# One dense transformer block on one core: where the gate-and-up stage makes its operand sums, and what is prepared before each stage begins

## The chip, the cores and the metric

The kernel runs on one core of a Trainium2 chip. The metric is the device time of one execution in microseconds (us); the times of the kernel before are from three runs. The engines are TensorE (PE: matmul, with its weight load PEld), VectorE (DVE), ScalarE (ACT), GpSimd (POOL) and SyncE (SP), which here issues nearly all DMAs.

## The reference

One layer over 2048 latent tokens of width 1024, with 256 context tokens in front: a modulated norm, one input projection shared by gated linear attention and differential attention, an output projection, and a gated feed-forward part of hidden width 2816. All of it is float32. The change touches what stands behind the attention:

```python
def swiglu(h, w_in, w_out):
    gate, up = jnp.split(h @ w_in, 2, axis=-1)
    return (jax.nn.silu(gate) * up) @ w_out
...
x = x + gt1 * (mixed @ w_out)
x = x + gt2 * swiglu(modulate(x, norm2_g, sh2, sc2), w_ffn_in, w_ffn_out)
```

(The last two lines are a short form.)

## The kernel before, in words

Every float32 operand is split in two: `split` lets ScalarE copy the value in reduced precision (`hi`, line 87) and VectorE subtract that from it (`lo`, line 84). A product is then three matmuls (`mm3`, lines 91 to 93: hi·hi, hi·lo, lo·hi), mostly 128x128 stationary by 512 moving columns. The helper `mul` is line 78, `add` line 81, `sub` line 84, whichever engine runs them. On TensorE instructions stand in the order of the code (`manual_schedule`); on the other engines a scheduler orders them, and each engine works through its list in order. Tiles come from pools with a fixed number of buffers, so a load or a split waits until the earlier user of its buffer is done.

Stages 1 to 3 (projections, linear attention, differential attention; to about 1519 us) are not edited.

*Output projection* (lines 897 to 1066). The eight 128x1024 chunks of `w_out` are loaded, multiplied by the gate `gt1` on GpSimd and split. `main(lt)` computes one token tile, from lt = 15 down to 0: two halves of 512 columns, each 8 chunks of `mm3`, taken in the order 4, 5, 6, 7, 0, 1, 2, 3. Between its chunks `prep` makes the next tile's operand (norms, transposes) and `mod2(g)` the normalised, transposed input `h2` of the feed-forward part for two token tiles. Groups 4 to 7 stay on chip in the blocks `hb`, groups 0 to 3 are stored. `mod2(0)`, the last, runs behind the last `main`. `early_ops` makes slot 0 and two sums.

*Gate and up* (lines 1068 to 1153). Tokens in two halves of 1024; for each half 22 blocks of 128 hidden columns. A block is a two-by-two product (gate and up by two token groups of 512; two halves of the inner dimension of 1024) done with seven products instead of eight. The moving operands are slots `o0` to `o6`, 128x2048 each, hi and lo: four pieces of `hb` and three sums, made by `rest_ops` before the half's first block. The stationary operands are seven 128x512 pieces `wh`, `wl`: three pieces of the weight tile `wi` and four sums of them (`s2`, `s3`, `a21`), which GpSimd makes. A product is 4 x `mm3` = 12 matmuls into a PSUM bank `p`; VectorE and ScalarE combine the banks to gate and up in tiles `e`, `g` and store the result to `act`. A block is 84 matmuls, the stage 44 x 84 = 3696.

*Down stage* (lines 1155 to 1192). For each half of the 1024 output columns (`dd`) the 22 weight chunks `wo` are loaded, multiplied by the gate `gt2` (GpSimd and VectorE in turn) and split into `wot`; for each of 16 token tiles `ar` (128x2816) is loaded from `act`, split into `ah`, `al`, and 22 x `mm3` = 66 matmuls with 512 columns make one result, to which `x1t` is added (2 x 16 x 66 = 2112 matmuls). The pool of `wot` has 22 + 6 buffers, that of `wo` 4.

Of the kernel before, what the change touches and what calls it, by code (L numbers as in the profile page):

```python
# [11 lines left out]
F32 = mybir.dt.float32  # L12
# [21 lines left out]
GA, GB, EQB, DEFER = 2, 5, 2, 4  # L34
PREP, MOD = (0, 7, 13), (1, 8, 10, 12, 14)
# [14 lines left out]
def dit_block(ctx: ExitStack, tc: tile.TileContext, x, c, cx, c_ctx, w_mod, b_mod, norm1_g, w_in, gate_up,  # L50
# [839 lines left out]
    with ExitStack() as st:  # L890
# [25 lines left out]
        wo = [tuple(wp.tile([P, D], F32R, name=f"wo{u}_{k}") for u in "hl") for k in range(KT)]  # L916
        for k in range(KT):
            w = xp.tile([P, D], F32, name="xt", tag="xt")
            load(w, w_out[0, k * P:(k + 1) * P, :])
            mul(w, w, gt1, G)  # L920
            split(wo[k][0], wo[k][1], w)
        def gla_out(lt, mixt):
# [141 lines left out]
        for _ in mod2(0):  # L1064
            pass
# [3 lines left out]
        SEQ_P = ((0, 0, True), (1, 1, True), (0, 2, False), (2, 3, True), (3, 4, True), (2, 5, False), (3, 6, False))  # L1069
# [6 lines left out]
        ep = st6.enter_context(tc.tile_pool(name="s5e", bufs=2, side="right", reuse_waits="tile"))  # L1076
# [155 lines left out]
```

## Time and profile before

| | |
|---|---|
| time, median of three runs | 3206.38 us (3201.48, 3206.38, 3211.32) |
| time of the profiled execution | 3207.87 us |
| its span, first to last instruction | 3206.1 us |
| mean granted TensorE clock | 0.977 of full speed |
| busy share: PE, DVE, ACT, POOL | 96%, 67%, 44%, 25% |

The profile shows one execution. A busy share is a mean over all stages; what an edit in one stage can give is read from that stage's own stretch. Times in the views count from the first instruction of the span. "Released by" names the instruction whose end let another one begin.

### The profile page before, as it was taken

The page shows a single profiled execution, that of the slowest core. Times are in us where ns is not written, and L with a number is a line of the kernel's source. Part 1 is how long each engine was busy: PE and PEld are TensorE (multiplying, and loading weights), DVE is VectorE, ACT ScalarE, POOL GpSimd, SP SyncE. Part 2 cuts the span into 40 slices and gives each one's busy share as a digit, 9 for nine tenths or more (in the row PEclk, how much of TensorE's full clock was granted, in tenths as well). Part 3 has the DMA queues.
Part 4 walks back from the last instruction along what each step waited for, and adds up shares of the span by engine and source line. Part 5 has one row for each costly group of instructions (what it writes and reads, how often), then busy time and mean ns, then how long its engine had stood idle before and what let it go on. Part 6 is the DMA issues. An engine that isn't in the chain of part 4 may idle for free.

```text
span 3206.1 us, 41971 instructions
## 1 busy us (share of the span) xinstructions
PE 3061.8 (96%) x15124; PEld 2497.9 (78%) x15124; DVE 2144.5 (67%) x4608; ACT 1411.2 (44%) x2169; POOL 796.0 (25%) x506
## 2 busy tenths in 40 slices
PE   7999999999989999999699799998999997999999
PEld 4888788888867777777588588887788885887787
DVE  7888668878899999998786744446554445323322
ACT  5333466666567777776333333334233333212211
POOL 2111000000056556654321322222322222100000
PEclk9999999999999999999899899999999998999999
DMA  8965511211332222211556332222222325434331
GB/s 307 302 225 200 165 68 66 93 63 62 95 83 65 63 66 57 57 52 45 176 169 199 110 87 86 79 79 65 74 80 83 87 73 180 153 135 158 125 136 66
DMA packets 316769, 363.46 MB, mean 113 GB/s; under 512 B 25361, under 2 KB 258258, under 8 KB 305810
## 3 DMA queue, kind: packets, MB, share of 16 engines
q1 hardware_dynamic: 313970, 351.35, 34.4%
q0 software_dynamic: 2304, 8.39, 0.8%
q8 instruction: 119, 1.95, 0.2%
q10 hardware_dynamic: 288, 1.05, 0.1%
q14 instruction: 88, 0.72, 0.1%
HBM read 249.96 MB, written 110.76 MB: 113 GB/s over the span
## 4 chain that ended last, share of the span: by engine, by line
PE 64%; DVE 3%; DMA 2%; POOL 1%; issue 1%; ACT 1%; SPq 0%; POOLq 0%; DVEq 0%; ACTq 0%
PE p L93 9%; PE p L92 9%; PE p L91 9%; PE o L92 6%; PE o L93 6%; PE o L91 6%; PE t L818 4%; PE s L773 4%; PE s L774 4%; PE o L841 3%; PE mm L92 2%; PE mm L91 2%; PE mm L93 2%; DMA wo<-in_w_ffn_out 1%; POOL p L81 0%
## 5 line engine op out<-in xcount | busy, mean ns | idle before, releaser
L81 POOL TENSOR_TENSOR p<-p,p 128x1152 f32<-128x1152 f32 x128 | 366.3, 2882 | 289.7 <-DVE p L805 174.7
L775 DVE TENSOR_SCALAR_CACHE_REDUCE p<-s 128x512 f32<-128x512 f32 (+1 forms) x640 | 382.0, 631 | 13.5 <-PE s L774 9.5
L91 PE MATMUL mm<-wh,hh 128*128 128x512 f32 (+2 forms) x976 | 379.0, 388 | 0.0
L93 PE MATMUL mm<-wh,hl 128*128 128x512 f32 (+2 forms) x976 | 355.0, 364 | 0.1
L92 PE MATMUL mm<-wl,hh 128*128 128x512 f32 (+2 forms) x976 | 354.4, 363 | 0.0
L81 DVE TENSOR_TENSOR e<-p,e 128x512 f32<-128x512 f32 x220 | 152.1, 691 | 279.9 <-PE p L93 279.9
L781 ACT ACTIVATE p<-p,nm 128x2304 f32<-128x2304 f32 x128 | 283.8, 2217 | 44.5 <-DVE nm L779 44.5
L91 PE MATMUL o<-wot,ah 128*128 128x512 f32 x704 | 279.6, 397 | 19.7 <-ACT wot L87 19.6
L92 PE MATMUL o<-wot,ah 128*128 128x512 f32 x704 | 280.2, 398 | 8.7 <-DVE wot L84 8.7
L773 PE MATMUL s<-k,qh 128*128 128x512 f32 (+1 forms) x640 | 275.7, 435 | 9.6 <-DVE p L775 8.7
L93 PE MATMUL o<-wot,al 128*128 128x512 f32 x704 | 278.0, 395 | 0.0
L87 ACT ACTIVATE wh<-wi 128x512 fp32r<-128x512 f32 x176 | 111.1, 632 | 326.0 <-PE p L92 247.3
L774 PE MATMUL s<-k,ql 128*128 128x512 f32 (+1 forms) x640 | 234.4, 373 | 1.3 <-DMA ql<-ql 1.3
L87 ACT ACTIVATE ah<-ar 128x2816 fp32r<-128x2816 f32 x32 | 81.9, 2559 | 327.5 <-PE o L92 312.1
L84 POOL TENSOR_TENSOR s<-wi 128x512 f32<-128x512 f32 x88 | 113.7, 1292 | 427.6 <-DVE wl L84 419.4
L93 PEld LDWEIGHTS mm<-wh,hl 128*128 128x128 f32 x976 | 185.1, 190 | 30.2 <-DVE hl L84 0.5
L91 PEld LDWEIGHTS mm<-wh,hh 128*128 128x128 f32 x976 | 186.1, 191 | 23.1 <-issue 0.5
L81 DVE TENSOR_TENSOR x1t<-o,x1t 128x512 f32<-128x512 f32 x32 | 22.1, 691 | 271.3 <-PE o L93 271.3
L92 PEld LDWEIGHTS mm<-wl,hh 128*128 128x128 f32 x976 | 186.1, 191 | 21.4 <-issue 0.5
L87 ACT ACTIVATE wh<-s 128x512 fp32r<-128x512 f32 x132 | 83.4, 632 | 247.1 <-PE p L92 231.0
L84 DVE TENSOR_TENSOR wl<-s,wh 128x512 fp32r<-128x512 f32 x132 | 93.1, 705 | 126.1 <-ACT wh L87 125.9
L91 PEld LDWEIGHTS o<-wot,ah 128*128 128x128 f32 x704 | 134.6, 191 | 52.9 <-ACT wot L87 24.8
(287 smaller groups left out, 7557.9 us busy)
## 6 DMA issues: line engine op xcount, KB each, us to landing
wi<-in_w_ffn_in SPq DMA_DIRECT2D x88, 512.0 KB, 5.4
ar<-act SPq DMA_DIRECT2D x32, 1408.0 KB, 5.8
act<-e SPq DMA_DIRECT2D x88, 256.0 KB, 2.6
wm<-in_w_mod SPq DMA_DIRECT2D x32, 512.0 KB, 5.0
xt<-in_x SPq DMA_DIRECT2D x30, 512.0 KB, 3.9
wr<-in_w_in SPq DMA_DIRECT2D x12, 1024.0 KB, 7.5
wo<-in_w_ffn_out SPq DMA_DIRECT2D x44, 256.0 KB, 3.8
hdh<-hh SPq DMA_DIRECT2D x9, 1024.0 KB, 4.8
```

Of the source, the lines that this page charges most:

```text
L81: (eng or V).tensor_tensor(out=o, in0=a, in1=b, op=ALU.add)
L84: (eng or V).tensor_tensor(out=o, in0=a, in1=b, op=ALU.subtract)
L87: S.activation(hi, src, AF.Copy)
L91: T.matmul(ps, a[0], b[0], start=start, stop=False, **how)
L92: T.matmul(ps, a[0], b[1], start=False, stop=False, **how)
L93: T.matmul(ps, a[1], b[0], start=False, stop=stop, **how)
L773: T.matmul(ps[:, 0:n], qd[0][c_][:, qc], ks_[h, c_][:, o0:o0 + n], start=True, stop=False)
L774: T.matmul(ps[:, 0:n], qd[1][c_][:, qc], ks_[h, c_][:, o0:o0 + n], start=False, stop=True)
L775: V.tensor_scalar(out=pr[c_][:, o0:o0 + n], in0=ps[:, 0:n], scalar1=1.0, scalar2=-3.0e38, op0=ALU.mult, op1=ALU.max, accum_out=mx[:, j:j + 1])
L781: S.activation(pr[c_], pr[c_], AF.Exp, bias=nm, accum_out=l)
L818: T.transpose(pt[:, i, :], as_[bi][i][:, kt * P:(kt + 1) * P], ident)
L841: T.matmul(po[:, 0:nq, :], v[0], at[0], start=kt == 0, stop=kt == NKT - 1)
```

## The change

- *Output projection.* The first half of the columns takes the chunks in the order 4, 5, 6, 7, 0, 1, 2, 3, the second in the order 3, 2, 4, 5, 6, 7, 0, 1, and the loads are issued in the first of these orders. The pool of the split weights moves to the other side of the memory, below the pools of loads and sums. Two pads shift the tiles of this stage.
- *Before gate and up.* `early_ops` makes slots 0 and 1; its two sums go from GpSimd to VectorE. `mod2(0)` is gone from the end of the stage: `last_group` does its work inside the second block of gate and up, from `x1` read back from memory.
- *Gate and up.* All sums, of weights and of token blocks, are on VectorE. The code makes a product's weights three products ahead (`AHEAD`), with 7 instead of 6 pairs of buffers. The slots of the first half are made one by one ahead of their products; those of the second half are rebuilt one by one, slot i right after product i of the first half's last block (n = 21). The second half runs its column blocks in reverse, and its first block uses the weights of the block before again. The pad ahead of the weight pools grows from 24 to 56 floats for each partition. In the built programs the weight tiles `wh`, `wl` began 384 bytes past a multiple of 512 in a partition, and begin 256 past one after; the slots begin 256 past one in both. The tiles `wot`, `ah`, `al` of the down stage before begin 256 past one as well.
- *Down stage.* Two token tiles are worked on together, so that each weight chunk serves 6 matmuls in a row instead of 3; `ar` comes in halves of 11 chunks (128x1408). The gate `gt2` is no longer multiplied into the weights but, on VectorE, into each result. Weights of the second `dd` are made in the pairs 5 and 7.

Of the diff, the core:

```diff
+ORD0, ORD1 = (4, 5, 6, 7, 0, 1, 2, 3), (3, 2, 4, 5, 6, 7, 0, 1)
+PAD4 = 16
+AHEAD = 3
...
-        slots = {0: slot(sl0, 0)}
+        slots = {i: slot(sl0, i) for i in range(2)}
...
+        pad = st1.enter_context(tc.tile_pool(name="s4pad", bufs=1, side="right"))
+        G.memset(pad.tile([P, 56], F32, name="pad"), 0.0)
...
+        pad = st1.enter_context(tc.tile_pool(name="s4pad2", bufs=1, side="right"))
+        G.memset(pad.tile([P, PAD4], F32, name="pad"), 0.0)
         ph = st1.enter_context(tc.tile_pool(name="s4h", bufs=2, side="right", reuse_waits="tile"))
-        wp = st1.enter_context(tc.tile_pool(name="s4w", bufs=1, side="right", reuse_waits="tile"))
+        wp = st1.enter_context(tc.tile_pool(name="s4w", bufs=1, reuse_waits="tile"))
...
-        wo = [tuple(wp.tile([P, D], F32R, name=f"wo{u}_{k}") for u in "hl") for k in range(KT)]
-        for k in range(KT):
+        wo = {k: tuple(wp.tile([P, D], F32R, name=f"wo{u}_{k}") for u in "hl") for k in ORD1}
+        for k in ORD0:
...
-            order = (4, 5, 6, 7, 0, 1, 2, 3)
-            for j in range(2):
+            for j, order in enumerate((ORD0, ORD1)):
...
                 for k in order:
-                    mm3(ps, (mh[:, k, :], ml[:, k, :]), (wo[k][0][:, js], wo[k][1][:, js]), k == 4, k == 3)
-                    if k == 3:
+                    mm3(ps, (mh[:, k, :], ml[:, k, :]), (wo[k][0][:, js], wo[k][1][:, js]), k == order[0], k == order[-1])
+                    if k == order[-1]:
                         add(x1[:, js], ps, xt[:, js])
...
         def early_ops():
-            split(slots[0][0], slots[0][1], hb[0][0])
-            sub(hb[0][1], hb[1][1], hb[0][1], G)
-            add(hb[0][0], hb[0][0], hb[0][1], G)
+            (b11, b12), (b21, b22) = hb
+            split(*slots[0], b11)
+            sub(b12, b22, b12)
+            add(b11, b11, b12)
+            split(*slots[1], b11)
...
-        for _ in mod2(0):
-            pass
...
-        G.memset(pad.tile([P, 24], F32, name="pad"), 0.0)
+        G.memset(pad.tile([P, 56], F32, name="pad"), 0.0)
         rwp = st6.enter_context(tc.tile_pool(name="s5r", bufs=2, side="right", reuse_waits="tile"))
-        opp = st6.enter_context(tc.tile_pool(name="s5w", bufs=6, side="right", reuse_waits="tile"))
+        opp = st6.enter_context(tc.tile_pool(name="s5w", bufs=7, side="right", reuse_waits="tile"))
...
-        def rest_ops(hb, slots, first):
-            (b11, b12), (b21, b22) = hb
-            if not first:
-                slots[0] = slot(sl0, 0)
-                sub(b12, b22, b12, G)
-                split(*slots[0], b11)
+        def rebuild(blocks, i, fresh):
+            (b11, b12), (b21, b22) = blocks
+            if fresh:
+                slots[i] = slot(sl0 if i < 2 else sl1, i)
+            if i == 1 and fresh:
                 add(b11, b11, b12)
-            for i, src in ((1, b11), (2, b21), (3, b12), (4, b12), (5, b21), (6, b22)):
-                if i == 4:
-                    sub(b12, b22, b11, V if first else G)
-                if i == 5:
-                    sub(b21, b21, b11, G)
-                slots[i] = slot(sl1, i)
-                split(*slots[i], src)
...
+            if i == 4:
+                sub(b12, b22, b11)
+            if i == 5:
+                sub(b21, b21, b11)
+            split(*slots[i], (b11, b11, b21, b12, b12, b21, b22)[i])
+
+        def last_group():
+            xt = h2p.tile([P, 2, D], F32, name="lx", tag="hb00")
+            xn = h2p.tile([P, 2, D], F32, name="lxn", tag="hb01")
+            ht = h2p.tile([P, KT, 256], F32, name="lht", tag="hb10")
+            ss = tmp.tile([P, 2], F32, name="lss", tag="lss")
+            for t in range(2):
+                load(xt[:, t, :], x1_d[t])
+            for t in range(2):
+                S.activation(xn[:, t, :], xt[:, t, :], AF.Square, accum_out=ss[:, t:t + 1])
+            rs = rms_rstd(tmp, ss, D, 2, "l")
+            for t in range(2):
+                V.tensor_scalar(out=xn[:, t, :], in0=xt[:, t, :], scalar1=rs[:, t:t + 1], scalar2=None, op0=ALU.mult)
+            yield
...
+                if kp % 2:
...
+        work = [(1, j) for j in range(NH)] + [(0, j) for j in reversed(range(NH))]
+        raws, kept, sums = {}, {}, {}
...
+        def weights(n, i):
+            if n == NH:
+                return
...
+            a11, s2, a12, s3, a21, a22, _ = sums[n]
+            if i == 1:
+                s2 = tmp.tile([P, 4, P], F32, name="s2", tag="s2")
+                s3 = tmp.tile([P, 4, P], F32, name="s3", tag="s3")
+                sub(s3, a11, a21)
+                add(a21, a21, a22)
+                sub(s2, a21, a11)
+                sums[n] = a11, s2, a12, s3, a21, a22, s2
+            if i == 6:
+                sub(s2, a12, s2)
+            kept[n, i] = [opp.tile([P, 4, P], F32R, name=f"w{u}", tag=f"w{u}") for u in "hl"]
+            split(*kept[n, i], sums[n][i])
+
+        banks, e = [None] * 4, {}
...
+            wh_, wl_ = kept[n - 1, i] if n == NH else kept[n, i]
+            for k in range(4):
...
+        flat = [(n, i) for n in range(len(work)) for i in range(7)]
         with tc.manual_schedule(engines=MS):
-            for half in (1, 0):
-                rest_ops(hb, slots, half == 1)
...
-                    sub(s3, a11, a21, G)
-                    add(a21, a21, a22, G)
-                    sub(s2, a21, a11, G)
...
-                            sub(s2, a12, s2, G)
-                            srcs[6] = s2
-                        wh_, wl_ = wsplit(srcs[i])
...
+            fetch(0)
+            fetch(1)
+            for m in range(AHEAD):
+                weights(*flat[m])
+            late = last_group()
+            for m, (n, i) in enumerate(flat):
+                if n == 0 and i < 5:
+                    rebuild(hb, i + 2, True)
+                if m + AHEAD < len(flat):
+                    weights(*flat[m + AHEAD])
+                if n == 1 and i < 6:
+                    next(late, None)
+                if n == 3 and i == 0:
+                    hb0 = h2_blocks()
+                    for k in range(2):
+                        for b in range(2):
+                            load(hb0[k][b], h2_d[k][b])
+                if n == 6 and i == 0:
+                    sub(hb0[0][1], hb0[1][1], hb0[0][1])
+                ps = product(n, i)
+                finish(n, i, ps)
+                if n == NH - 1:
+                    rebuild(hb0, i, True)
+                if i == 6 and n + 2 < len(work) and n + 2 != NH:
+                    fetch(n + 2)
...
+        downs, chunks = {}, {}
...
+        def down_weights(dd, j):
+            w = wrp.tile([P, 512], F32, name="wo", tag="wo")
+            load(w, w_fo[0, j * P:(j + 1) * P, dd * 512:(dd + 1) * 512])
+            wt = wop.tile([P, 2, 512], F32R, name="wot", tag="wot")
+            split(wt[:, 0], wt[:, 1], w)
...
+            load(ar, act_d[lt // 8][lt // 4 % 2][:, lt % 4, c_ * HC:(c_ + 1) * HC])
+            chunks[lt, c_] = [acp.tile([P, HC, P], F32R, name=f"a{u}", tag=f"a{u}") for u in "hl"]
+            split(*chunks[lt, c_], ar)
...
+        pairs = [(dd, lt) for dd in range(2) for lt in (*range(8, 16, 2), *range(0, 8, 2))]
...
-                    n += 1
-                    ar = pool.tile([P, NH, P], F32, name="ar", tag="ar")
-                    load(ar, act_d[lt // 8][lt // 4 % 2][:, lt % 4])
-                    ah, al = [pool.tile([P, NH, P], F32R, name=f"a{u}", tag=f"a{u}") for u in "hl"]
-                    split(ah, al, ar)
...
-                        for j in range(NH):
-                            w = wrp.tile([P, 512], F32, name="wo", tag="wo")
...
-                            mul(w, w, gt2[:, js], G if j % 2 else V)
-                            wt = wop.tile([P, 2, 512], F32R, name="wot", tag="wot")
-                            split(wt[:, 0], wt[:, 1], w)
...
+                ps, x1t = [], []
+                for t in range(2):
...
+                for c_ in range(2):
...
+                    if n == 0:
+                        for j in range(c_ * HC, (c_ + 1) * HC):
+                            down_weights(0, j)
...
+                    nx = (n, 1) if c_ == 0 else (n + 1, 0)
+                    if nx[0] < len(pairs):
+                        for t in range(2):
+                            tokens(pairs[nx[0]][1] + t, nx[1])
+                    for j in range(c_ * HC, (c_ + 1) * HC):
+                        ah, al = zip(*[chunks[lt + t, c_] for t in range(2)])
+                        for t in range(2):
+                            mm3(ps[t], (ah[t][:, j - c_ * HC, :], al[t][:, j - c_ * HC, :]), downs[dd, j], j == 0, j == NH - 1)
+                        if n == 5 and j < 6:
+                            down_weights(1, j)
+                        if n == 7 and j + 6 < NH:
+                            down_weights(1, j + 6)
+                for t in range(2):
+                    o = op_.tile([P, 512], F32, name="ot", tag="ot", bufs=2)
+                    mul(o, ps[t], gt2[:, js])
+                    add(x1t[t], o, x1t[t])
+                    store(out[0, (lt + t) * P:(lt + t + 1) * P, js], x1t[t])
```

Where instructions go, at three places. On SyncE, between attention and output projection (`md`, `mx`, `on` belong to the attention's result; `xt` are load buffers), before:

```order
L960 DMA mx<-md_13_203 128x128
L860 DMA md_0_238<-on 128x128
...
L860 DMA md_3_241<-on 128x128
L960 DMA mx<-md_13_219 128x128
...
L960 DMA mx<-md_13_251 128x128
L919 DMA xt<-in_w_out 128x1024 x8
L962 DMA xt<-in_x 128x1024 x2
```

and now:

```order
L938 DMA Ub<-ub_178 64x512
L921 DMA gt_16425<-gt_83 128x1024
L926 DMA xt<-in_w_out 128x1024 x4
L863 DMA md_4_242<-on 128x128
...
L968 DMA mx<-md_13_203 128x128
L863 DMA md_0_238<-on 128x128
...
L968 DMA mx<-md_13_251 128x128
L926 DMA xt<-in_w_out 128x1024 x4
L944 DMA qq<-qi_132 128x512
```

Four of the eight loads have moved in front of the last two groups of `md` stores; the other four stand where all eight stood.

On VectorE, at the end of the output projection and the start of gate and up (`wl` are low parts of weights, `o1l` to `o6l` those of the slots, `hb` token blocks, `s` weight sums, `ht` the output of `mod2`), before:

```order
L84 TENSOR_TENSOR wl<-s_18905,wh 128x512
L1034 TENSOR_SCALAR ht<-tp,A_77,B_78 128x256 x4
L84 TENSOR_TENSOR wl<-wi,wh 128x512 x2
L1034 TENSOR_SCALAR ht<-tp,A_77,B_78 128x256 x4
L84 TENSOR_TENSOR o1l<-hb_16380,o1h 128x2048
L84 TENSOR_TENSOR o2l<-hb_16382,o2h 128x2048
L84 TENSOR_TENSOR o3l<-hb_16381,o3h 128x2048
L84 TENSOR_TENSOR o6l<-hb_16383,o6h 128x2048
L84 TENSOR_TENSOR hb_16381<-hb_16383,hb_16380 128x2048
L84 TENSOR_TENSOR o5l<-hb_16382,o5h 128x2048
L84 TENSOR_TENSOR o4l<-hb_16381,o4h 128x2048
```

and now:

```order
L87 TENSOR_TENSOR wl<-wi,wh 128x512
L87 TENSOR_TENSOR s_18850<-wi 128x512
L84 TENSOR_TENSOR wi<-wi 128x4x128
L87 TENSOR_TENSOR s_18849<-wi 128x512
L87 TENSOR_TENSOR o2l<-hb_16382,o2h 128x2048
L87 TENSOR_TENSOR wl<-s_18849,wh 128x512
...
L87 TENSOR_TENSOR o3l<-hb_16381,o3h 128x2048
L87 TENSOR_TENSOR wl<-wi,wh 128x512
L84 TENSOR_TENSOR e_18883<-p_18893,e_18883 128x512
L87 TENSOR_TENSOR hb_16381<-hb_16383,hb_16380 128x2048
L87 TENSOR_TENSOR wl<-wi,wh 128x512
L87 TENSOR_TENSOR hb_16382<-hb_16382,hb_16380 128x2048
```

The `ht` pieces and `o1l` are gone from here, three weight sums and one more block sum have come, and the slots stand between the weights instead of in one row.

On ScalarE, from the last block of gate and up into the down stage (`e`, `g` results of the block, `ah` high parts of tokens, `wot` of weights), before:

```order
L1137 ACTIVATE g_25065<-p_25016 128x512
L87 ACTIVATE ah<-ar 128x2816
L1150 ACTIVATE e_25029<-e_25029 128x512
L87 ACTIVATE wot<-wo 128x512 x5
L87 ACTIVATE ah<-ar 128x2816
L87 ACTIVATE wot<-wo 128x512 x18
```

and now:

```order
L1179 ACTIVATE g_25044<-p_24995 128x512
L1190 ACTIVATE e_25008<-e_25008 128x512
L90 ACTIVATE ah<-ar 128x1408
L90 ACTIVATE wot<-wo 128x512 x4
L90 ACTIVATE ah<-ar 128x1408 x3
L90 ACTIVATE wot<-wo 128x512 x10
```

The first token piece now stands behind the last activation of `e`, is half as long, and three more follow after four weight chunks.

## Rows read from the trace of the kernel before

**Rows 1.** Table of stretches: busy time (instructions) of each engine, clock, DMA share, GB/s.

```profile
core 0: us, PE busy (x) PEld busy (x) DVE busy (x) ACT busy (x) POOL busy (x), PEclk, DMA share, GB/s
...
1519.00:1559.00 40.00, 11.79 (x36) 8.33 (x36) 29.53 (x27) 12.11 (x21) 24.37 (x8) 0.62 0.56 183
...
1767.60:1778.60 11.00, 4.00 (x18) 3.09 (x17) 9.26 (x14) 5.88 (x12) 8.04 (x7) 0.71 0.12 49
1778.60:1818.80 40.20, 26.72 (x87) 20.48 (x86) 32.10 (x24) 16.95 (x15) 13.35 (x7) 0.74 0.46 157
1818.80:2230.40 411.60, 410.19 (x1766) 332.24 (x1765) 214.84 (x293) 134.03 (x215) 113.79 (x83) 1.00 0.28 81
2230.40:2266.60 36.20, 22.45 (x85) 17.76 (x84) 31.03 (x25) 11.03 (x14) 14.87 (x8) 0.76 0.16 44
...
2676.40:2681.70 5.30, 0.32 (x2) 0.00 (x0) 2.08 (x3) 1.26 (x2) 0.00 (x0) 0.85 0.93 316
2681.70:2727.10 45.40, 27.93 (x67) 16.52 (x68) 32.52 (x35) 15.79 (x24) 17.39 (x12) 0.72 0.62 216
...
2951.50:2977.60 26.10, 20.14 (x67) 14.12 (x66) 17.88 (x19) 8.92 (x12) 8.15 (x5) 0.80 0.46 157
```

**Rows 2.** Timeline of TensorE: start, duration; gate and up, then down stage.

```profile
1901.35 0.39 PE L91 MATMUL p<-o1h,wh 128*128 128x512 f32 x1
...
1920.87 0.39 PE L91 MATMUL p<-o1h,wh 128*128 128x512 f32 x1
...
3194.83 0.39 PE L92 MATMUL o<-wot,ah 128*128 128x512 f32 x1
...
3201.63 0.39 PE L92 MATMUL o<-wot,ah 128*128 128x512 f32 x1
```

**Rows 3.** Timeline into the output projection; the last row from the view of tile p.

```profile
1522.79 19.80 SPq L919 DMA_DIRECT2D xt<-in_w_out  x8
...
1526.67 24.37 POOL L78 TENSOR_TENSOR xt<-xt,gt 128x1024 f32<-128x1024 f32 x8 [18.61 <-DMA xt<-in_w_out]
1529.05 1.06 ACT L87 ACTIVATE woh<-xt 128x1024 fp32r<-128x1024 f32 x1 [3.87 <-POOL xt L78]
...
1542.29 0.80 PE L91 MATMUL mm<-woh,mh 128*128 128x512 f32 x1 [23.28 <-ACT woh L87]
...
L81 POOL TENSOR_TENSOR p<-p,p x8: 2644/2861/3092, 1461.8 to 1493.2; 128x1152 f32<-128x1152 f32 x8
```

**Rows 4.** Timeline of the first block of gate and up.

```profile
1788.44 2.29 DVE L84 TENSOR_TENSOR o1l<-hb,o1h 128x2048 fp32r<-128x2048 f32 x1 [6.01 <-DMA h<-ht]
...
1793.01 6.58 POOL L84 TENSOR_TENSOR hb<-hb,hb 128x2048 f32<-128x2048 f32 x1 [13.54 <-DVE o2l L84]
...
1795.05 6.68 DVE L84 TENSOR_TENSOR o6l<-hb,o6h 128x2048 fp32r<-128x2048 f32 x1
...
1805.93 0.49 PE L91 MATMUL p<-o4h,wh 128*128 128x512 f32 x1 [4.33 <-ACT o4h L87]
```

**Rows 5.** Groups of instructions, 1850 to 2200 us: count, busy us, mean ns, idle before.

```profile
L81 DVE TENSOR_TENSOR e<-p,e 128x512 f32<-128x512 f32 x90 | 62.3, 692 | 119.6 <-PE p L93 119.6
L84 DVE TENSOR_TENSOR wl<-wi,wh 128x512 fp32r<-128x512 f32 x72 | 58.5, 813 | 0.0
L84 POOL TENSOR_TENSOR s<-wi 128x512 f32<-128x512 f32 x36 | 46.4, 1289 | 181.2 <-DVE wl L84 181.2
```

**Rows 6.** Waits, 2230 to 2268 us: total us, times, longest.

```profile
PE p L93 <- DVE wl L84: 13.7, 1, 13.7
```

**Rows 7.** Into the down stage: timeline, waits, and the view of tile wo.

```profile
2678.87 0.52 SPq L1152 DMA_DIRECT2D act<-e  x1
...
PE o L91 <- ACT wot L87: 14.9, 6, 5.0
...
DMA to landing us min/median/max: 2.9/3.3/5.8
```

**Rows 8.** Timeline of the end.

```profile
3202.28 0.69 DVE L81 TENSOR_TENSOR x1t<-o,x1t 128x512 f32<-128x512 f32 x1 [14.27 <-PE o L93]
```

More of the change, by code (lines that the diff above doesn't have):

```diff
@@ new lines, in rebuild @@
+        def rebuild(blocks, i, fresh):
[3 more added lines that the diff above has]
+            if i == 1 and fresh:
+                add(b11, b11, b12)
+            if i == 4:
[16 more added lines that the diff above has]
+            yield
+            for kp in range(KT // 2):
+                ps = ps5.tile([P, 2, 256], F32, name="p1", tag="p1")
+                for j in range(2):
+                    for t in range(2):
+                        k = 2 * kp + j
+                        T.transpose(ps[:, j, t * P:(t + 1) * P], xn[:, t, k * P:(k + 1) * P], ident)
+                for j in range(2):
+                    k = 2 * kp + j
+                    V.tensor_scalar(out=ht[:, k, :], in0=ps[:, j, :], scalar1=A2[:, k:k + 1], scalar2=B2[:, k:k + 1],
+                                    op0=ALU.mult, op1=ALU.add)
+                if kp % 2:
+                    store(h2_d[kp // 2][0][:, :, 0:256], ht[:, 2 * kp - 2:2 * kp + 2, :])
+                yield
@@ new lines, in dit_block, with fetch @@
+        work = [(1, j) for j in range(NH)] + [(0, j) for j in reversed(range(NH))]
+        raws, kept, sums = {}, {}, {}
+        def fetch(n):
+            j = work[n][1]
+            w = rwp.tile([P, KT, 2, P], F32, name="wi", tag="wi")
+            for u in range(2):
+                load(w[:, :, u, :], w_fi[0, :, u * HID + j * P:u * HID + (j + 1) * P].rearrange("(k p) n -> p k n", p=P))
+            raws[n] = w
+        def weights(n, i):
+            if n == NH:
+                return
+            if i == 0:
+                w = raws.pop(n)
+                a11, a12, a21, a22 = [w[:, 4 * k:4 * k + 4, u, :] for u in range(2) for k in range(2)]
+                sums[n] = a11, None, a12, None, a21, a22, None
+            a11, s2, a12, s3, a21, a22, _ = sums[n]
[10 more added lines that the diff above has]
+            split(*kept[n, i], sums[n][i])
@@ new lines, in dit_block, with product @@
+        banks, e = [None] * 4, {}
+        def product(n, i):
+            bk, new = SEQ_P[i]
+            if new:
+                banks[bk] = ps5.tile([P, 512], F32, name=f"p{bk}", tag=f"p{bk}")
+            ps = banks[bk]
+            wh_, wl_ = kept[n - 1, i] if n == NH else kept[n, i]
+            for k in range(4):
+                mm3(ps, (wh_[:, k, :], wl_[:, k, :]), (slots[i][0][:, k, :], slots[i][1][:, k, :]),
+                    new and k == 0, k == 3, skip_group_check=not new)
+            return ps
@@ new lines, in etile, with finish @@
+        def etile(nm, bufs):
+            e[nm] = ep.tile([P, 512], F32, name=nm, tag=nm, bufs=bufs)
+            return e[nm]
+        def finish(n, i, ps):
+            half, j = work[n]
+            if i == 0:
+                S.activation(etile("e1", 2), ps, AF.Copy)
+            elif i == 1:
+                add(e["e1"], ps, e["e1"])
+            elif i == 2:
+                S.activation(etile("g1", 1), ps, AF.Silu)
+            elif i == 3:
+                add(etile("e2", 1), ps, e["e1"])
+            elif i == 4:
+                add(e["e2"], ps, e["e2"])
+            elif i == 5:
+                add(etile("e3", 1), ps, e["e1"])
+                mul(e["e3"], e["e3"], e["g1"])
+                store(act_d[half][0][:, :, j, :], e["e3"].rearrange("p (t n) -> p t n", n=P))
+            else:
+                add(e["e1"], ps, e["e1"])
+                S.activation(e["e1"], e["e1"], AF.Silu)
+                mul(e["e2"], e["e2"], e["e1"])
+                store(act_d[half][1][:, :, j, :], e["e2"].rearrange("p (t n) -> p t n", n=P))
@@ L1163, in dit_block @@
+        wop = st.enter_context(tc.tile_pool(name="s6w", bufs=NH + 6, reuse_waits="tile"))
         ps6 = st.enter_context(tc.tile_pool(name="s6ps", bufs=4, space=PSUM, reuse_waits="tile"))
@@ new lines, in dit_block @@
+                ps, x1t = [], []
+                for t in range(2):
+                    ps.append(ps6.tile([P, 512], F32, name="o", tag="o"))
+                    x1t.append(op_.tile([P, 512], F32, name="x1t", tag="x1t"))
+                    load(x1t[t], x1_d[lt + t][:, js])
+                for c_ in range(2):
+                    if n == 0 and c_ == 0:
+                        for t in range(2):
+                            tokens(lt + t, 0)
+                    if n == 0:
[7 more added lines that the diff above has]
+                        ah, al = zip(*[chunks[lt + t, c_] for t in range(2)])
+                        for t in range(2):
+                            mm3(ps[t], (ah[t][:, j - c_ * HC, :], al[t][:, j - c_ * HC, :]), downs[dd, j], j == 0, j == NH - 1)
[3 more added lines that the diff above has]
+                            down_weights(1, j + 6)
```

82 lines of the change are left out of this document (10 added, 72 removed).

## The prediction

> **What bounds the kernel now.** I read the table of stretches first. In the middle of the gate-and-up stage TensorE is busy 410.19 of 411.60 us at a granted clock of 1.00 [rows 1]; inside a stage only fewer matmuls or a shorter matmul can help. The same table shows where TensorE is not full: six stretches around the hand-overs, busy 11.79 of 40.00, 4.00 of 11.00, 26.72 of 40.20, 22.45 of 36.20, 27.93 of 45.40 and 20.14 of 26.10 us, with clocks from 0.62 to 0.80, besides 5.30 us with almost no matmul [rows 1]. The change removes no matmul: 3696 in the gate-and-up stage (44 blocks of 84), 2112 in the down stage (32 results of 66). So I price the hand-overs one by one, plus one term for the pace.
>
> **Pace of a matmul.** Start to start, 84 matmuls of the gate-and-up stage, one whole block, take 1920.87 − 1901.35 = 19.52 us, 232.4 ns each; 30 of the down stage take 3201.63 − 3194.83 = 6.80 us, 226.7 ns each [rows 2]. Both run at full clock with 512 columns and three matmuls for each pair of operands. One difference I could find is in the pools' addresses: in the gate-and-up stage the stationary tiles `wh`, `wl` begin 384 bytes past a multiple of 512, the moving slots 256 past; in the down stage both begin 256 past. The pad raised from 24 to 56 floats moves `wh`, `wl` by 128 bytes, to 256 past. I take 226.7: 5.7 ns × 3696 = **−21 us**; bounds 0 and −21. The Trainium skill's page "TensorE: Matmul & The Clock Gate" (section "Wait — 56ns, not 53.3ns?") gives a warm start-to-start of N/2.4 GHz plus about 2.5 ns, 215.7 ns at 512 columns, and knows of no address in it. By that rule the term would be 0; the trace has 226.7 and 232.4, so something outside the rule is in it here. The output projection's tiles are moved too, for at most 1.5 us; taken as 0.
>
> **Into the output projection.** Before, SyncE issues the eight `w_out` loads at 1522.79; GpSimd multiplies them by the gate from 1526.67 for 24.37 us, 3.05 each; ScalarE's high part takes 1.06 and TensorE's first matmul starts at 1542.29 [rows 3], because the loop uses chunks 4 to 7 first and they come last. The stretch ends at 1559. After, loads come in the order of use and the first four stand ahead of the last attention traffic. Their buffers lie over attention tiles which the last GpSimd addition `p` (started 1493.2, 2.9 us [rows 3]) leaves free, so four multiplies run by about 1508. ScalarE's high parts stand behind its head-output work until about 1521. The second four loads still stand behind the `md` stores, issued at about 1523.7; the first lands after 3.9 us as before (1522.79 to 1526.67), 4 × 3.05 ends at 1539.5, high and low parts at 1541.8, and three matmuls later the first half is done, about 1542.8 instead of 1558.9. **−16 us**; bounds 0 (the second four set the end after all) and −22 (ScalarE and loads let go as early as the mixing permits).
>
> **Into gate and up.** Before, after the last projection matmul TensorE does the norm's transposes (11.00 us) and then spends 40.20 us on a first block worth 19.52: 31.7 lost, and 1.4 more in the next stretch (410.19 busy of 411.60): 33.1 [rows 1]. The cause is in the second group: `o1l` starts at 1788.44 for want of a DMA, `o6l` takes 6.68 us while GpSimd's `hb` sum runs (2.29 without), and TensorE waits 4.33 us for `o4h` [rows 4]. After, slots 0 and 1 are ready beforehand; the norm of the last group is in block 1, so no transpose stands in front of product 0. Then VectorE is a serial chain: four 128x512 sums and splits at 0.7, six 128x2048 pieces at 2.3. By its order `o4l` is done at 1786.6 and product 4 waits about 5 us, products 5 and 6 about 2 each; product 6 ends about 1797 against an ideal of 1787, 10 late; the transposes in block 1, which wait for two loads and a square, may cost 3 more. With 2 us of half clock that is 15 lost: **−18.1**; bounds −30 and −8.
>
> **Within a block.** The four sums leave GpSimd, 1.29 us each [rows 5], for VectorE. VectorE then has 7 splits, 4 sums and 7 finishing steps, 18 × 0.69 = 12.4 us of a block of 19.0 [rows 5]. The wait added: each finishing step stands at VectorE's head until its product ends. Queued behind it are the weights of the product four further on, which TensorE wants 8 us later; that is cover enough, so 0. Without it every late split would cost its 0.7 us.
>
> **Change of halves.** 22.45 busy in 36.20, one block of 19.52: 16.7 lost, 13.7 of it one wait for a low part queued behind four slot rebuilds [rows 1, 6]. After, the block order is mirrored, so block 22 reuses the weights of block 21, and slot i is rebuilt right after product i, six products ahead of its use. Left are about 2.5 us at product 2, where two 1.9 us slot copies and the bank's copy share ScalarE, and 1 at product 5: **−13.2**; bounds −16.7 and −5.
>
> **Into the down stage.** 5.30 us and then 45.40 for a first token tile of 66 × 226.7 = 15.0: 35.7 lost [rows 1]. The last `act` store is issued at 2678.87, TensorE waits 14.9 us for `wot` high parts and the loads land 2.9 to 5.8 us after their issue [rows 7]. After, two tiles share each weight chunk, so 22 chunks feed 132 matmuls instead of 66 (1.36 us of TensorE per chunk instead of 0.68), the gate multiply is gone from the chunk (on VectorE and GpSimd half each), four chunks are fetched inside the last block, and a token load is half as long. Against that, three of the first four token loads stand behind the last act store (about 2.5 us after the last product), as do ScalarE's and VectorE's pieces behind `e2`. First matmul at about +6, second tile's at +9.8, of which 1.1 us is matmul: 8.7 lost; four for the later chunks behind two token loads; one or two at half clock: 14. **−21.6**; bounds −31 and −12.
>
> **Change of column halves, end.** 26.10 − 15.0 = 11.1 lost [rows 1]. After, six spare weight buffers are filled in pair 5 and the rest in pair 7 as chunks come free, one per six matmuls, 1.36 us, against 0.6 us of ScalarE: 0 left, **−11.1**; bounds −11.1 and −5. At the end one addition of 0.69 [rows 8] becomes two multiplies and two additions: **+1.5**.
>
> Sum: −16 − 18.1 − 21 − 13.2 − 21.6 − 11.1 + 1.5 = −99.5, from the profiled execution's 3207.87: 3108.4. That execution was 1.5 above the median, so **3107**.
>
> **Rivals.** (a) *The pace stays.* Something other than the address sets 232.4 (the slots' own place, or that weights and slots of this stage are written by engines at the same time). For it: an undisturbed row that shares all but the address is missing. Against it: the down stage at 226.7 has ScalarE and VectorE at work too. 3107 + 21 = 3128. (b) *The hand-overs close almost wholly.* If VectorE's pieces keep ahead, 12 less into gate and up, 9 less into down, 2.5 less at the halves: 3107 − 23.5 = 3083. (c) *The early `w_out` loads bring nothing*, because ScalarE or the second four loads come as late as now: 3123. (d) *VectorE becomes the bound*: slower. To use up 100 us over 44 blocks a block must take 2.3 us more than 19.0, so 21.3, which is 1.19 us for each of 18 operations. For it: beside GpSimd's sums the `wl<-wi` splits mean 0.81 instead of 0.69 [rows 5]; the chain of sum, split and finishing is serial. Against it: GpSimd no longer works in this stage, and 0.69 is 12.4 of 19.0. At that point the time is 3206, at 1.3 us an operation (23.4 a block) about 3300.
>
> **How the numbers follow.** Forecast 0.55, (a) 0.15, (b) 0.15, (c) 0.10, (d) 0.05. The range 3080 to 3137 takes in (a), (b) and (c), with 9 us above (a) for its own spread, and leaves out (d) and the outer bounds of several terms at once. A change below 0.3%, 10 us, is about what a measurement of this kernel cannot tell from none. Only (d) reaches there: faster 0.96, same 0.01, slower 0.03, the rest of (d) still being faster.
>
> **What would show it.** Right: matmuls of the middle blocks 226.7 ns apart, a block 19.0 us; GpSimd idle in gate and up; VectorE at 60 to 65% there; no wait for a `wl` low part over 3 us at the change of halves; TensorE full across the change of column halves; stretches from the last product of one stage to the second block of the next with losses near 15 and 14 us. Wrong: 232 ns again (a); TensorE waiting for VectorE in every block (d); the first output-projection half ending at 1559 again (c). The least sure terms are the two of 15 and 14 left behind, read off an order and not off a trace.

## The result: 3118.23 us, 2.7% less; one term of seven missed by 11 us

The changed kernel takes 3118.23 us (median of four runs, 3116.53 to 3120.88), the kernel before 3205.65 in the same four rounds; the ratio is 0.9727 with a 95% interval of 0.971 to 0.9744. The forecast was 3107, the range 3080 to 3137. The profiled execution took 3118.64 us, 89.2 below that of before, where −99.5 was forecast.

The table of stretches of the changed kernel, with the columns of [rows 1]:

```profile
1518.00:1560.00 42.00, 29.04 (x124) 21.52 (x123) 29.96 (x39) 17.37 (x34) 11.48 (x6) 0.80 0.45 144
...
1762.40:1794.20 31.80, 23.04 (x85) 16.73 (x84) 28.41 (x28) 17.43 (x20) 0.53 (x1) 0.89 0.33 116
1794.20:1816.00 21.80, 21.47 (x102) 17.30 (x102) 21.17 (x38) 9.69 (x16) 0.00 (x0) 1.00 0.63 216
1816.00:2189.00 373.00, 373.00 (x1647) 308.88 (x1646) 234.01 (x351) 121.02 (x197) 0.00 (x0) 1.00 0.30 88
2189.00:2195.00 6.00, 3.75 (x17) 2.79 (x16) 6.00 (x4) 3.18 (x2) 0.00 (x0) 1.00 0.00 0
2195.00:2238.00 43.00, 42.85 (x182) 34.92 (x181) 34.60 (x42) 16.96 (x22) 0.00 (x0) 0.96 0.34 105
...
2620.00:2626.60 6.60, 0.49 (x4) 0.07 (x2) 1.96 (x3) 2.61 (x4) 0.00 (x0) 0.90 0.90 263
2626.60:2662.00 35.40, 33.30 (x129) 25.58 (x130) 23.21 (x28) 19.23 (x26) 0.00 (x0) 0.87 0.88 303
...
2860.00:2885.00 25.00, 25.00 (x112) 20.71 (x111) 12.63 (x14) 7.61 (x9) 0.00 (x0) 1.00 0.61 219
```

The last projection matmul now starts at 1762.20 and product 0 follows at 1762.43; before, the stage ended at 1767.60 and its first block began 11 us later. GpSimd computes nothing from there on, and VectorE is at 234 of 373 us in the middle of gate and up, 63%. The change of column halves (2860 to 2885) shows no gap. At the change of halves (2189 to 2238) one gap is left, 3.75 busy of 6.00 us. Most of what remains stands in the first stretch and at the two starts of a stage.

Of TensorE's timeline, two matmuls of the changed kernel that are 84 apart; they answer to the first two of [rows 2]:

```profile
1900.31 0.39 PE L94 MATMUL p<-o3h,wh 128*128 128x512 f32 x1
...
1919.35 0.39 PE L94 MATMUL p<-o3h,wh 128*128 128x512 f32 x1
```

A block takes 19.04 us, 226.7 ns a matmul, as the down stage.

The timeline from the attention's tail into the output projection, answering to [rows 3]:

```profile
1495.48 9.52 POOL L81 TENSOR_TENSOR xt<-xt,gt 128x1024 f32<-128x1024 f32 x4
...
1496.42 0.68 DVE L87 TENSOR_TENSOR al<-t,ah 128x512 fp32r<-128x512 f32 x1
...
1498.77 6.39 DVE L940 SCALAR_TENSOR_TENSOR S<-S,Tall,Ub 64x128 f32<-64x128 f32 x3
...
1506.74 0.79 PE L95 MATMUL o<-al,vh 128*128 128x512 f32 x1 [5.14 <-DVE al L87]
...
1530.82 3.73 SPq L926 DMA_DIRECT2D xt<-in_w_out  x4
...
1534.29 9.44 POOL L81 TENSOR_TENSOR xt<-xt,gt 128x1024 f32<-128x1024 f32 x4 [21.50 <-DVE wol L87]
...
1536.71 7.16 DVE L940 SCALAR_TENSOR_TENSOR S<-S,Tall,Ub 64x128 f32<-64x128 f32 x3
...
1546.29 0.79 PE L95 MATMUL mm<-wol,mh 128*128 128x512 f32 x1 [7.97 <-DVE wol L87]
...
1551.79 0.69 DVE L84 TENSOR_TENSOR xt<-mm,xt 128x512 f32<-128x512 f32 x1
```

Twice four gate products run on GpSimd, and twice three small pieces `S` on VectorE, which belong to the linear attention's state, last until the products end: 6.39 and 7.16 us for three. TensorE waits 5.14 us in the attention and 7.97 in the projection for what VectorE does next; the last row is the end of the projection's first half. The second four loads are issued at 1530.82, behind an attention that ended later; before, all eight were issued at 1522.79 [rows 3].

### The profile page after: what moved, and what is told of

The parts are those of the page before. It is cut to its first block, busy times and chain, and to the rows that moved or that the text cites. A ratio compares the mean times of both kernels' runs of the same rounds, so it can differ in the third digit from the quotient of the medians.

```text
span 3116.9 us, 41971 instructions
## 1 busy us (share of the span) xinstructions
PE 3023.3 (97%) x15124; PEld 2486.5 (80%) x15124; DVE 2203.2 (71%) x4820; ACT 1411.9 (45%) x2195; POOL 495.6 (16%) x304
## 5 line engine op out<-in xcount | busy, mean ns | idle before, releaser
L94 PE MATMUL o<-wot,ah 128*128 128x512 f32 x704 | 275.4, 391 | 6.8 <-ACT wot L90 6.1
L95 PE MATMUL o<-wot,ah 128*128 128x512 f32 x704 | 275.2, 391 | 0.9 <-DVE wot L87 0.9
L90 ACT ACTIVATE ah<-ar 128x1408 fp32r<-128x1408 f32 x64 | 85.3, 1374 | 315.9 <-PE o L95 311.5
L87 DVE TENSOR_TENSOR al<-ar,ah 128x1408 fp32r<-128x1408 f32 x64 | 101.4, 1621 | 132.0 <-ACT ah L90 132.0
L821 PE MATMUL t<-ident,p 128*128 128x128 f32 x1152 | 174.7, 274 | 2.0 <-POOL p L84 2.0
L821 PEld LDWEIGHTS t<-ident,p 128*128 128x128 f32 x1152 | 142.7, 142 | 37.4 <-issue 4.1
L776 PEld LDWEIGHTS s<-k,qh 128*128 128x128 f32 x640 | 121.7, 190 | 59.7 <-DVE p L778 18.1
```

The source lines that it names most:

```text
L87: (eng or V).tensor_tensor(out=o, in0=a, in1=b, op=ALU.subtract)
L90: S.activation(hi, src, AF.Copy)
L94: T.matmul(ps, a[0], b[0], start=start, stop=False, **how)
L95: T.matmul(ps, a[0], b[1], start=False, stop=False, **how)
L776: T.matmul(ps[:, 0:n], qd[0][c_][:, qc], ks_[h, c_][:, o0:o0 + n], start=True, stop=False)
L821: T.transpose(pt[:, i, :], as_[bi][i][:, kt * P:(kt + 1) * P], ident)
```

## The experiments

Each kernel is the changed kernel with one edit, except the first; times are medians, ratios are to the kernel before in the same rounds. In the diffs, "-" is the kernel that is edited.

**Pace: the place of the weights.** The first kernel is the one before, with one number changed:

```diff
-        G.memset(pad.tile([P, 24], F32, name="pad"), 0.0)
+        G.memset(pad.tile([P, 56], F32, name="pad"), 0.0)
```

> The kernel before with one number changed: the pad ahead of the gate-and-up weight pools 56 floats instead of 24, so that wh and wl begin 256 instead of 384 bytes past a multiple of 512. If the place of the weights sets the pace: a middle block 19.04 us instead of 19.52, 226.7 ns a matmul, the time 21 us less (ratio 0.9934). If the pace came from GpSimd's sums or anything else of the change: a block stays 19.52, ratio 1.000.

3186.83 us, ratio 0.9937 (0.992 to 0.9953). Two matmuls of its TensorE timeline that are 84 apart:

```profile
1899.73 0.39 PE L91 MATMUL p<-o2h,wh 128*128 128x512 f32 x1
...
1918.77 0.39 PE L91 MATMUL p<-o2h,wh 128*128 128x512 f32 x1
```

19.04 us, with GpSimd's sums and the rest of the code as before. The reverse, 24 floats in the changed kernel:

> The changed kernel with the gate-and-up pad back at 24 floats. If the place of the weights sets the pace: a middle block 19.52 us, the time 21 us more than the changed kernel, about 3139 (ratio to before 0.979). If not: 19.04 and 3118 (0.973).

3138.84 us, ratio 0.979 (0.9776 to 0.9805): the 20.6 us are back. GpSimd at the sums again, with the new pad:

```diff
-                sub(s3, a11, a21)
-                add(a21, a21, a22)
-                sub(s2, a21, a11)
+                sub(s3, a11, a21, G)
+                add(a21, a21, a22, G)
+                sub(s2, a21, a11, G)
...
-                sub(s2, a12, s2)
+                sub(s2, a12, s2, G)
```

> The changed kernel with the four weight sums of each block on GpSimd again, the block sums staying on VectorE. If the place of the weights sets the pace, a middle block stays 19.04 us and the time within 10 us of 3118, with VectorE's share lower and a different loss in the first block. If an idle GpSimd sets the pace, a block is 19.52 us and the time about 3139.

3125.33 us, ratio 0.9744 (0.973 to 0.9759). On its timeline the first matmul of a product and the same one a block later, and from its waits between 1762 and 1830 us (total, times, longest):

```profile
1900.11 0.39 PE L94 MATMUL p<-o1h,wh 128*128 128x512 f32 x1
...
1919.15 0.39 PE L94 MATMUL p<-o1h,wh 128*128 128x512 f32 x1
```

```profile
ACT wh L90 <- POOL s L87: 18.2, 4, 11.0
```

The pace stays 19.04 us. By the times this kernel can hardly be told from the changed one (the intervals overlap); the profiled executions, 3127.02 and 3118.64 us, are 8.4 apart. Of that 7.6 lie at the starts, where the weights' high parts wait for GpSimd's sums: the first two blocks take 35.59 and 23.37 us instead of 31.81 and 21.75, the two at the change of halves 44.86 instead of 42.71. Two other places, with pads of 88 and 120 floats:

> The changed kernel with a pad of 88 floats: wh and wl begin 128 bytes past a multiple of 512, the slots still 256 past. If weights and slots must lie equally far past such a multiple, or an odd multiple of 128 is the bad place, a middle block is 19.52 us; if only 384 past is bad, 19.04.

> The changed kernel with a pad of 120 floats: wh and wl begin at a multiple of 512 bytes, the slots 256 past one. If weights and slots must lie equally far past such a multiple: a middle block 19.52 us. If only odd multiples of 128 are bad: 19.04.

3135.04 and 3119.06 us, one profiled execution each. The timelines, first of the kernel with 88 floats, then of that with 120, again 84 matmuls apart:

```profile
1900.01 0.41 PE L94 MATMUL p<-o3h,wh 128*128 128x512 f32 x1
...
1919.53 0.41 PE L94 MATMUL p<-o3h,wh 128*128 128x512 f32 x1
```

```profile
1900.41 0.39 PE L94 MATMUL p<-o3h,wh 128*128 128x512 f32 x1
...
1919.45 0.39 PE L94 MATMUL p<-o3h,wh 128*128 128x512 f32 x1
```

With the slots 256 past a multiple of 512 bytes, weights 384 and 128 past one run at 232.4 ns, weights 256 past and at one at 226.7. So they need not lie equally far; of the four places the two odd multiples of 128 are slow. The pad moves the other tiles behind it too (the raw weights `wi`, the sums, `e`). Of all these TensorE reads only `wh` and `wl`, so I take their place as the cause; they were not moved apart from the rest. Whether the slots' place matters too was not tried.

**Into the output projection.** Two kernels take the gate product from GpSimd, one by leaving it out of the weights and multiplying each result by it on VectorE (`gt1` then keeps a buffer of its own):

```diff
-            mul(w, w, gt1, G)
...
+                        mul(ps, ps, gt1[:, js])
                         add(x1[:, js], ps, xt[:, js])
```

> The changed kernel, but the gate gt1 is not multiplied into the eight w_out chunks on GpSimd; VectorE multiplies each output-projection result by it instead (32 products of 0.7 us, 22 us in a stage of 202 us in which VectorE is busy 149). If GpSimd's early products hold up VectorE in the attention's tail and the second four make the chain: the last attention matmul is back from 1522.8 to about 1515.5, the 8 us wait for a low part is gone, the first half of the projection ends near 1537 instead of 1551, the time 12 to 16 us less, about 3104 (0.968). If the delay has another cause (loads, ScalarE's order): 1522.8 again and 3115 to 3119; if VectorE becomes late in the projection: above 3118.

3107.86 us, ratio 0.9688 (0.9673 to 0.9702), 10 us less than the changed kernel where 12 to 16 were expected. The other one (`mul(w, w, gt1)`) has it on VectorE:

> The changed kernel with the eight gate products of w_out on VectorE instead of GpSimd, loads at the same place. If two engines at once are the cause, VectorE's S pieces take 0.35 us each again, the attention ends near 1516 to 1518 and the first half of the projection near 1542; time about 3109 (0.970). If VectorE's own work in the tail is what holds it up, the attention ends as late as now or later, and the time is 3118 or more.

3107.11 us, ratio 0.9687 (0.9672 to 0.9701). Groups of VectorE from 1490 to 1523 us (count, busy us, mean ns, idle before): the `S` pieces of the changed kernel, then of the kernel with the gate on the output, then of the one with the product on VectorE.

```profile
L940 DVE SCALAR_TENSOR_TENSOR S<-S,Tall,Ub 64x128 f32<-64x128 f32 x4 | 7.3, 1855 | 0.1
```

```profile
L939 DVE SCALAR_TENSOR_TENSOR S<-S,Tall,Ub 64x128 f32<-64x128 f32 x4 | 1.2, 354 | 0.1
```

```profile
L81 DVE TENSOR_TENSOR xt<-xt,gt 128x1024 f32<-128x1024 f32 x4 | 4.8, 1215 | 0.0
...
L940 DVE SCALAR_TENSOR_TENSOR S<-S,Tall,Ub 64x128 f32<-64x128 f32 x4 | 1.2, 352 | 0.1
```

The loads stand where they stood; without GpSimd beside it a piece takes 0.35 us again. The last attention matmuls with `at` start at 1514.76 and 1514.20 instead of 1522.32. VectorE has more to do in the second kernel and is done sooner. That GpSimd's products hold it up is shown by the `S` pieces; what of the 10 to 11 us comes from a product taking 1.2 instead of 2.4 us on VectorE is not separated. The third edit moves the pool of the split weights:

```diff
-        wp = st1.enter_context(tc.tile_pool(name="s4w", bufs=1, reuse_waits="tile"))
+        wp = st1.enter_context(tc.tile_pool(name="s4w", bufs=1, side="right", reuse_waits="tile"))
```

> The changed kernel with the pool of the split w_out back on the other side, so that the load buffers lie where they lay before. If the early loads cost the attention its 7 us: the attention ends near 1515.5 again, the eight products are one chain behind 1522.8, the first half of the projection ends near 1554 (the loads being in the order of use), the time 2 to 4 us above 3118. If the early loads bring what was forecast and something else is late: the first half ends 15 us later than now, about 3133.

3104.07 us, ratio 0.9681 (0.9664 to 0.9697), 14 us below the changed kernel; both expectations failed, because the edit did the opposite of what I took it for. All eight loads, not four, are now issued ahead of the last `md` stores, from 1487.56 to 1512.22; I take it that with this pool out of the way the load buffers lie where room is free early. It is thus the test of "all early". Its VectorE groups from 1490 to 1523 us, its first projection matmul, and its stretch behind that:

```profile
L87 DVE TENSOR_TENSOR wol<-xt,woh 128x1024 fp32r<-128x1024 f32 x7 | 14.9, 2123 | 0.0
```

```profile
1527.67 0.50 PE L94 MATMUL mm<-woh,mh 128*128 128x512 f32 x1 [0.34 <-ACT mh L999]
```

```profile
1530.00:1560.00 30.00, 30.00 (x149) 24.99 (x148) 20.18 (x52) 12.30 (x42) 3.92 (x4) 1.00 0.56 168
```

The attention still ends as late, since a split of 1.22 us takes 2.12 beside GpSimd, but then every weight is ready: TensorE is full from 1530 to 1560, and the first addition of a projection result starts at 1535.08 instead of 1551.79. Both edits together:

> Both edits together: all eight w_out loads early (the pool of the split weights on the other side) and no gate product on GpSimd (gt1 multiplied into the projection's results on VectorE). If GpSimd's products beside VectorE were what held up the attention's tail, and late weights what interrupted the first half: the attention ends near 1515 to 1517 instead of 1522, the projection starts near 1521 and runs through, the time 5 to 7 us below the kernel with early loads alone and 10 below the one with the gate moved alone, about 3098 (0.966). If the attention's tail is held up by the split of the weights itself (ScalarE and VectorE), or the 22 us of products make VectorE late in the projection: 3104 or more.

3099.08 us (five runs, 3094.51 to 3101.74), ratio 0.9659 (0.9642 to 0.9677), the lowest time here. The same views of it:

```profile
L87 DVE TENSOR_TENSOR wol<-xt,woh 128x1024 fp32r<-128x1024 f32 x8 | 9.7, 1217 | 0.5 <-ACT woh L90 0.5
```

```profile
1519.62 0.47 PE L94 MATMUL mm<-woh,mh 128*128 128x512 f32 x1
```

```profile
1530.00:1560.00 30.00, 30.00 (x159) 25.07 (x159) 23.32 (x56) 10.57 (x33) 5.19 (x5) 1.00 0.53 171
```

The projection starts 8 us earlier than with early loads alone. By the times the two cannot be told apart (the intervals overlap); the profiled executions, 3096.23 and 3101.29, differ by 5 us, as much as runs of one kernel do.

**Into gate and up.** The norm of the last group back at the end of the projection:

```diff
+        for _ in mod2(0):
+            pass
         st1.close()
...
-            late = last_group()
...
-                if n == 1 and i < 6:
-                    next(late, None)
```

> The changed kernel with the norm of the last token group back at the end of the output projection, and no last_group in block 1. The forecast put the gain into gate and up on the slots being ready and on no transpose standing in front of product 0. If the transposes' place is worth its stretch: 8 to 11 us with almost no block matmul between the last projection matmul and product 0 come back, 2.7 us of block 1 go, and the first block keeps its 12.8 us loss or loses a little less: about 3124 to 3127. If VectorE's chain of slots sets the end anyway, product 4 starts when it does now plus VectorE's own 4 us for the norm: about 3122.

3120.96 us, ratio 0.9734 (0.9719 to 0.9748), not told apart from the changed kernel's 3118.23. In the trace product 0 starts 8.7 us behind the last projection matmul instead of 0.2, but the first block then takes 29.58 us instead of 31.81, and the second 19.04 instead of 21.75: 3.5 us in all. The waits of the changed kernel from 1761.5 to 1820 us, TensorE's alone, then two of this kernel from 1758 to 1820 us, then one row of VectorE's timeline in the changed kernel:

```profile
PE p L94 <- ACT wh L90: 3.0, 1, 3.0
...
PE p L95 <- DVE o4l L87: 2.3, 1, 2.3
...
PE p L96 <- DVE wl L87: 1.9, 2, 0.9
PE p L94 <- DVE e L84: 1.7, 2, 1.0
```

```profile
PE tp L1038 <- DVE n_rs L144: 4.3, 1, 4.3
...
PE p L95 <- DVE o2l L87: 2.4, 1, 2.4
```

```profile
1766.69 0.69 DVE L87 TENSOR_TENSOR s<-wi 128x512 f32<-128x512 f32 x1 [2.77 <-DMA x<-xt]
```

The four of the changed kernel wait for VectorE's slots, sums, low parts and finishing steps (`wh` waits for a sum). Transposes in front mostly move the waiting. But VectorE is not busy throughout: ahead of the first sum, behind the longest of the four waits, it stands idle for 2.77 us, by the profile until the store of the last projection result has landed. That the sum's buffer lies over the stored tile would explain it; no run moves it.

**Into the down stage.** One token tile at a time, the rest unchanged:

```diff
-        pairs = [(dd, lt) for dd in range(2) for lt in (*range(8, 16, 2), *range(0, 8, 2))]
+        pairs = [(dd, lt) for dd in range(2) for lt in (*range(8, 16), *range(8))]
...
-                for t in range(2):
+                for t in range(1):
...
-                        if n == 5 and j < 6:
+                        if n == 11 and j < 6:
...
-                        if n == 7 and j + 6 < NH:
+                        if n == 15 and j + 6 < NH:
```

> The changed kernel with one token tile at a time in the down stage; gate on the output, halves of 11 chunks and early weights stay. If two tiles for each weight chunk carry the gain into the down stage: a chunk must come every 0.68 us, loads and splits give one each 1.0 to 1.4 us, so 8 to 15 us more, 3126 to 3133. If the missing gate product carries it: within 4 us of 3118.

3132.05 us, ratio 0.9768 (0.9752 to 0.9785). The gate multiplied into the weights again, two tiles kept:

```diff
             load(w, w_fo[0, j * P:(j + 1) * P, dd * 512:(dd + 1) * 512])
+            mul(w, w, gt2[:, dd * 512:(dd + 1) * 512], G if j % 2 else V)
...
-                    o = op_.tile([P, 512], F32, name="ot", tag="ot", bufs=2)
-                    mul(o, ps[t], gt2[:, js])
-                    add(x1t[t], o, x1t[t])
+                    add(x1t[t], ps[t], x1t[t])
```

> The changed kernel with the gate gt2 multiplied into the down-stage weights again, GpSimd and VectorE in turn; two token tiles at a time stay. If the two tiles carry the gain: within 4 us of 3118, the change of column halves still without loss. If the gate product beside the splits was the bottleneck: a chunk takes 1.5 to 2 us as before, the first tile pair loses 10 us or more, 3128 or above.

3125.80 us, ratio 0.975 (0.9736 to 0.9765), between the two expectations. The interval overlaps the changed kernel's by a little; the traces separate the two. The first 132 matmuls of the stage, 29.92 us at full pace, take 60.33 us before, 36.17 in the changed kernel, 51.39 with one tile, 45.38 with gated weights. From the waits of the kernel with one tile (2620 to 2700 us), and the groups of the one with gated weights (2622 to 2660 us):

```profile
PE o L94 <- ACT wot L90: 12.5, 6, 6.0
...
PE o L95 <- DVE wot L87: 3.3, 7, 1.2
```

```profile
L87 DVE TENSOR_TENSOR wot<-wo,wot 128x512 fp32r<-128x512 f32 x18 | 16.7, 953 | 2.7 <-ACT wot L90 2.2
L81 POOL TENSOR_TENSOR wo<-wo,gt 128x512 f32<-128x512 f32 x7 | 13.2, 1898 | 425.0 <-DVE al L87 412.2 <-DMA wo<-in_w_ffn_out 4.5 <-DVE wo L81 4.3
...
L90 ACT ACTIVATE wot<-wo 128x512 fp32r<-128x512 f32 x18 | 10.8, 626 | 14.8 <-DVE wo L81 9.9 <-POOL wo L81 4.9
```

Taken back alone, the two tiles cost 15 us and the gate on the output 9, together about the 24 of the change; a kernel without both was not run, and neither were the early chunks and the shorter token loads taken out. The gate costs in two ways, whose shares are not separated: beside GpSimd's products a split takes 0.95 instead of 0.69 us, and ScalarE's high parts wait 14.8 us for products that stand ahead of them. The change of column halves stays without loss in both.

## Why the prediction was right, and where it was not

Measured from the two profiled executions, by stretches and by starts of matmuls:

| step | forecast | measured |
|---|---|---|
| into the output projection | −16 | −5.2 (end of the stage 1767.4 to 1762.2) |
| into gate and up | −18.1 | −17.6 (33.1 lost to 31.80 + 21.80 − 2 × 19.04 = 15.5) |
| pace | −21 | −21.1 (0.48 us × 44) |
| change of halves | −13.2 | −12.1 (16.7 lost to 4.6) |
| into the down stage | −21.6 | −23.2 (35.7 lost to 12.5) |
| change of column halves | −11.1 | −11.1 |
| end | +1.5 | +1.3 |

The sum is −89.0 against −89.2 measured. Six terms held to 1.6 us; two of the six, below, by parts that were not the forecast ones.

*The term that was mis-sized is that of the output projection*, −16 forecast and −5.2 measured. The step that failed is "four multiplies run by about 1508": they did, from 1495.48 for 9.52 us, and I let them cost nothing there, without naming what VectorE did meanwhile. It was in the attention's tail, on which TensorE waits. The attention ended 7 us later; the second four loads, forecast for 1523.7, were issued at 1530.82; and the same hold-up happened again at 1536.71, so that the first half ended at 1551.8 instead of 1542.8 (the forecast's own terms put its products' end at 1539.8, not 1539.5). Of the 7 us that the first half still gained on 1558.9, 5.2 are left at the stage's end; where the other 2 went no run shows. The sign of it was in the rows: `o6l` at 6.68 us instead of 2.29 while GpSimd's sum ran [rows 4], which I used for gate and up and not here. Removing the products from GpSimd gives 10 to 11 us back; having the second four loads early too gives 14 without touching the products. Rival (c), early loads that bring nothing, named the right place and a symptom: the second four loads did come late, but because what the first four let start got in the attention's way. In the kernel with the gate on the output, without those products, they were issued at 1523.27.

*Pace.* The price was right to 0.1 us, on a difference between two stages that I could not explain; one number in the kernel before then brought it alone. Rival (a) falls with it. The Trainium skill's page "TensorE: Matmul & The Clock Gate" (section "Wait — 56ns, not 53.3ns?") gives 215.7 ns at 512 columns with no word of the operands' place; the runs have 226.7 and 232.4, by the pad alone. What the 11 ns between 215.7 and 226.7 are made of, no run shows.

*Into gate and up.* The size was right, in part by luck. The part given to the transposes was not: with them in front again the start loses only 3.5 us. Of the 15.5 us lost, 2.7 are in the second block. In the first TensorE waits 4.9 us for weights, most of it at product 1, for which the forecast had nothing; product 4 waited 2.3 us for its slot, not 5; and `e` took 1.7. Of the other 4 us the clock can explain at most 3.5: its granted share was 0.89 over the 31.80 us, in part at its lower level, 1.2 GHz, to which it fell in the wait at product 1.

*Change of halves.* The size was right, the place was not: the wait left is 2.2 us at product 5 of the last block before the change, for a finishing step `e` of VectorE, and not at product 2 for ScalarE's copies. No run takes the mirrored order or the single rebuilds out, so their share rests on the stretches alone.

*Into the down stage.* Two of the reasons given were tried and hold, two tiles and the gate on the output; first matmul at +6.5 us for +6 forecast.

*Rival (d)*, a VectorE too slow for the block, did not come up: 63% busy for 65% forecast, no wait in the middle.

## What to carry to other kernels

Before letting work start early on GpSimd, look at what VectorE is doing for TensorE in that window, and price each of its instructions that takes both inputs from the on-chip memory SBUF at the length of a GpSimd one (the small `S` pieces, 1.86 us beside products of 2.38); moving a product behind the matmul may cost less than hiding it. If one stage runs its matmuls a few ns slower than another of the same shape, compare where the operands' tiles begin. Work taken from in front of a stage gains only what the next chain does not give back.

## What was not expected of the hardware

The start of the stationary operand in memory changes a matmul's pace by 2.5% in this stage: 226.7 ns at 0 and 256 bytes past a multiple of 512, 232.4 at 128 and 384, the moving operand at 256. And a VectorE piece of 64x128 elements, 0.35 us alone, took 1.86 us in the mean beside GpSimd's 128x1024 products of 2.38 us, a split of 128x1024 2.12 instead of 1.22: the small piece lost more than the large one. The Trainium skill's page "SBUF — State Buffer" (section "Who interferes with whom") says that a VectorE instruction with two inputs in this memory contends with GpSimd's reads; the runs agree, and add that a short instruction pays nearly the length of a GpSimd one. The low part `al` at 1496.42, which reads one input from TensorE's result memory, took 0.68 us in the midst of the first four products, as long as elsewhere (0.69 in the mean from 1490 to 1523 us).
